# Second expert products a step behind the first, on fourteen weight slots, with expert numbers on VectorE

## The chip, the core and the metric

The kernel runs on one core of one Trainium2 chip. The metric is device time in microseconds of one execution; the time before is the median of three runs. In the profile the engines are called PE (TensorE), DVE (VectorE), ACT (ScalarE), POOL (GpSimd) and SP (SyncE, which issues the weight loads).

## What is computed

Two decoder layers on 256 tokens of width 1024, in float32. Each layer has a mixer and then a channel mixer; the first layer's is dense, the second one's is a choice of two out of eight experts, and this change touches that one alone:

```python
def moe_swiglu(h, router_w, w1, w3, w2):
    logits = (h @ router_w).astype(jnp.float32)
    top_v, top_i = lax.top_k(logits, TOP_K)
    probs = jax.nn.softmax(top_v, axis=-1)
    gates = jnp.sum(jax.nn.one_hot(top_i, N_EXPERTS, dtype=jnp.float32) * probs[..., None], axis=-2)
    y = jnp.zeros_like(h)
    for e in range(N_EXPERTS):
        y = y + gates[..., e:e + 1] * swiglu(h, w1[e], w3[e], w2[e])
    return y
```

`swiglu` is `(silu(h @ w1) * (h @ w3)) @ w2`, with 2816 inner columns. A last RMS norm with the gain `final_g` follows.

## The kernel before, in words

**Places.** The experts are sorted by how many tokens chose them, expert 0 first. Places 0 to 2 (`WIDE = 3`) have 128 slots, places 3 to 6 have 64, place 7 has 32. Tokens beyond these would go through a slow branch at the end that does not run here. Which expert stands at a place is a number that `place` works out (L861 to L892), on GpSimd in seventeen small steps, and that SyncE reads into a register before it can load that place's weights (`of_place`, L914).

**Units and slots.** Each expert's weights are 33 units of 128 x 2048 floats, 1 MiB each: 11 of w1, 11 of w3, 11 of w2. `load` (L134) takes a slot from a rotating list of tiles and issues the unit's DMA on SP; SP issues in order, so a load that waits for its slot holds all later ones. At the start of the expert stage the list `once` gives fifteen slots for one use each: three of pool `ahead`, four of `more`, six of `rawp`, tile `xn` and tile `big`. After them only `more` and `rawp` rotate, ten slots. The memory of `ahead` becomes the activations `a_hi` and `a_lo` of all 22 inner blocks of one wide expert, `xn` becomes the scatter's tile and `big` the activations of a narrow expert.

**Wide and narrow.** For a wide place each half unit is split into two parts of reduced precision, `whi` by ACT (L145) and `wlo` by DVE (L146), and each block of the product is three matmuls (`mm3`, L157 to L159): a unit is twelve matmuls of 512 columns. The unit's slot is free when the second `wlo` is done. A narrow place uses the raw unit (L1050, L1099), two matmuls side by side on the columns of the array; its slot is free when PE has used it.

**Steps.** `steps(p)` gives an expert's work: six inner steps (`inner`, four units each, the last two; then `turn`, which transposes the 512 new columns and writes the activations), then three outer steps (`outer`) of four, four and three units of w2, and after the last `scatter`, which multiplies by the gate and adds the rows back to the residual `xs`. The string `TURNS` says whose turn it is: 0 is a step of the wide stream (places 0 to 2), 1 one of the narrow stream (3 to 7). What follows a step's products (`turn`, `prepare` for the next place, `scatter`) is written after the products of the next turn. Within this order a scheduler sets each engine's own sequence. `prepare` gathers a place's tokens by a one-hot product (L973) and modulates them; `HOLD_E` names how many splits may stand ahead of which of its steps.

**The end.** After the last step `last_norm` squares, takes the row norm and multiplies by the gain row `fgt` (L1223), and two DMAs write the output. The gain row is fetched by `last_gain`, behind the third wide expert's scatter.

## Time and profile before

| | |
|---|---|
| median of three runs | 1168.63 us (1168.21 to 1170.08) |
| the profiled execution | 1168.7 us, its span 1166.9 us, mean granted clock 0.979 |
| busy share of the span | PE 95%, weight loads on PE 64%, DVE 54%, ACT 44%, POOL 3% |
| moved by DMA | 395.69 MB, 339 GB/s over the span |

The span goes from the first instruction to the last; the time of an execution is 1.8 us longer. In the profile each group of instructions has its line in the kernel, its engine, its operation and its tiles; `raw` is a weight unit, `x_hi`, `x_lo` and `x_n` are gathered tokens, `po` and `pb` hold outer products. A busy PE need not be PE at its peak, since the ends of matmuls are modelled; two starts in a row tell its pace better. The expert stage begins at about 467 us and lasts to the end.

### The profile page before, as it was taken

What the parts mean: (1) busy time and instruction counts of PE and PEld (TensorE: products, weight loads), DVE (VectorE), ACT (ScalarE), POOL (GpSimd) and SP (SyncE); (2) the same over time, 40 slices, a digit from 0 to 9 for tenths busy, and PEclk for the clock granted to TensorE, in tenths of its full rate; (3) what the DMA queues carried; (4) which work ended last, traced back from release to release, by engine and by line L of the source; (5) the groups of instructions that cost most, each with busy time, mean ns of one, the idle gap of its engine ahead of it and who ended that gap; (6) DMA issues with size and microseconds to landing.
All of it is one profiled execution on the core that took longest, in us unless ns stands there. A gap on an engine that the chain in (4) does not pass through costs nothing.

```text
span 1166.9 us, 15801 instructions
## 1 busy us (share of the span) xinstructions
PE 1107.4 (95%) x6125; PEld 742.8 (64%) x6125; DVE 627.4 (54%) x818; ACT 518.3 (44%) x724; POOL 30.5 (3%) x69
## 2 busy tenths in 40 slices
PE   4899999999999999899999999999999999998993
PEld 2578779999777888686465445554455544655540
DVE  2668556757776765797135443353343633345442
ACT  2764444444437744786234333542342333434331
POOL 2000000000001000300000000000000000000000
PEclk9899999999999999899999999999999999998996
DMA  9977486858886447495999999999999999999994
GB/s 361 410 288 291 145 324 249 310 201 306 334 332 229 147 143 288 181 359 189 418 420 419 420 419 420 419 420 420 388 406 419 420 419 419 419 419 403 398 420 172
DMA packets 57182, 395.69 MB, mean 339 GB/s; under 512 B 8294, under 2 KB 8710, under 8 KB 9356
## 3 DMA queue, kind: packets, MB, share of 16 engines
q1 hardware_dynamic: 54272, 393.24, 84.2%
q10 hardware_dynamic: 2828, 1.37, 0.4%
q8 instruction: 50, 0.82, 0.3%
q14 instruction: 32, 0.26, 0.1%
HBM read 393.53 MB, written 1.05 MB: 338 GB/s over the span
## 4 chain that ended last, share of the span: by engine, by line
PE 88%; DMA 4%; ACT 3%; DVE 2%; POOL 1%; issue 1%; ACTq 0%; POOLq 0%; DVEq 0%; SPq 0%
PE pa L1050 17%; PE pa L158 8%; PE pa L157 8%; PE pa L159 8%; PE po L1099 7%; PE pa L406 6%; PE pa L407 6%; PE pa L408 6%; PE pb L158 4%; PE pb L159 4%; PE pb L157 4%; PE pm L226 2%; PE pb L261 2%; PE pm L973 2%; DMA bdx<-in_wx_dram 2%; ACT whi L145 2%
## 5 line engine op out<-in xcount | busy, mean ns | idle before, releaser
L146 DVE TENSOR_TENSOR wlo<-raw,whi 128x1024 fp32r<-128x1024 f32 x318 | 378.6, 1222 | 205.1 <-ACT whi L145 204.4
L145 ACT ACTIVATE whi<-raw 128x1024 fp32r<-128x1024 f32 x318 | 324.5, 1057 | 214.7 <-PE pa L407 90.2
L1050 PE MATMUL pa<-raw,x_n 128*64 128x512 f32 (+3 forms) x960 | 205.0, 562 | 0.0
L406 PE MATMUL pa<-wide_hi,whi 128*128 128x256 f32 x544 | 154.3, 284 | 0.2 <-DVE wide_hi L380 0.2
L407 PE MATMUL pa<-wide_lo,whi 128*128 128x256 f32 x544 | 153.5, 282 | 0.2 <-DVE wide_lo L381 0.2
L408 PE MATMUL pa<-wide_hi,wlo 128*128 128x256 f32 x544 | 153.5, 282 | 0.0
L1050 PEld LDWEIGHTS pa<-raw,x_n 128*64 128x64 f32 (+1 forms) x960 | 63.0, 131 | 106.7 <-issue 101.3
L158 PE MATMUL pa<-wlo,x_hi 128*128 128x512 f32 (+1 forms) x288 | 113.3, 394 | 3.7 <-DVE wlo L146 3.7
L157 PE MATMUL pa<-whi,x_hi 128*128 128x512 f32 (+1 forms) x288 | 110.7, 389 | 0.9 <-ACT whi L145 0.3
L159 PE MATMUL pa<-whi,x_lo 128*128 128x512 f32 (+1 forms) x288 | 109.9, 382 | 0.1
L406 PEld LDWEIGHTS pa<-wide_hi,whi 128*128 128x128 f32 x544 | 102.3, 188 | 6.4 <-issue 4.0
L407 PEld LDWEIGHTS pa<-wide_lo,whi 128*128 128x128 f32 x544 | 102.5, 189 | 1.6 <-issue 1.1
L408 PEld LDWEIGHTS pa<-wide_hi,wlo 128*128 128x128 f32 x544 | 102.5, 188 | 0.3 <-issue 0.3
L1099 PE MATMUL po<-raw,big 128*64 128x512 f32 (+1 forms) x440 | 93.4, 616 | 6.3 <-DMA raw<-in_m_dram 6.3
L1053 ACT ACTIVATE s<-pa 128x512 f32<-128x512 f32 (+1 forms) x30 | 16.9, 562 | 163.4 <-PE pa L1050 163.4
L158 PE MATMUL pb<-wlo,a_hi 128*128 128x512 f32 x176 | 71.6, 408 | 2.0 <-DVE wlo L146 2.0
L158 PEld LDWEIGHTS pa<-wlo,x_hi 128*128 128x128 f32 x288 | 55.3, 192 | 26.5 <-DVE wlo L146 6.7
L159 PE MATMUL pb<-whi,a_lo 128*128 128x512 f32 x176 | 69.8, 398 | 0.0
L157 PEld LDWEIGHTS pa<-whi,x_hi 128*128 128x128 f32 x288 | 55.3, 192 | 21.8 <-issue 7.7
L157 PE MATMUL pb<-whi,a_hi 128*128 128x512 f32 x176 | 60.8, 403 | 2.0 <-ACT whi L145 2.0
L1099 PEld LDWEIGHTS po<-raw,big 128*64 128x64 f32 (+1 forms) x440 | 25.4, 132 | 57.8 <-issue 49.8
L159 PEld LDWEIGHTS pa<-whi,x_lo 128*128 128x128 f32 x288 | 55.5, 193 | 10.0 <-DVE x_lo L986 0.8
(323 smaller groups left out, 1242.4 us busy)
## 6 DMA issues: line engine op xcount, KB each, us to landing
raw<-in_m_dram SPq DMA_DIRECT2D x263, 1024.0 KB, 10.6
raw<-in_ada_w_dram SPq DMA_DIRECT2D x48, 1024.0 KB, 7.3
raw<-in_f_dram SPq DMA_DIRECT2D x33, 1024.0 KB, 6.0
raw<-in_win_dram SPq DMA_DIRECT2D x20, 1024.0 KB, 6.3
raw<-in_wout_dram SPq DMA_DIRECT2D x8, 1024.0 KB, 6.1
xs<-in_x_dram SPq DMA_DIRECT2D x1, 1024.0 KB
big<-in_m_dram SPq DMA_DIRECT2D x1, 1024.0 KB
out_dram<-big SPq DMA_DIRECT2D x2, 512.0 KB, 3.2
```

What stands on the lines that cost most here:

```text
L145: act.activation(hi[:, :n], src, AF.Copy)
L146: dve.tensor_tensor(lo[:, :n], src, hi[:, :n].bitcast(F32), op=ALU.subtract)
L157: pe.matmul(ps, l_hi, r_hi, start=first, stop=False)
L158: pe.matmul(ps, l_hi, r_lo, start=False, stop=False)
L159: return pe.matmul(ps, l_lo, r_hi, start=False, stop=last)
L226: return pe.transpose(o, i, ident[:i.shape[0], :i.shape[0]])
L261: pe.matmul(ps[o:o + 32, :], cact[:, k, :], wi[:, h * 512:(h + 1) * 512], start=(j == 0), stop=(j == 3))
L406: pe.matmul(pv[:, b, :], wh, h_hi[:, k, :], start=(k == 0), stop=False)
L407: pe.matmul(pv[:, b, :], wh, h_lo[:, k, :], start=False, stop=False)
L408: pe.matmul(pv[:, b, :], wl, h_hi[:, k, :], start=False, stop=(k == KD - 1))
L1050: pe.matmul(ps[r:r + m, :n], x_n[:, k, :], w[:, kk * n:(kk + 1) * n], start=(k < js), stop=(k >= KD - js))
L1099: pe.matmul(acc[r:r + m, :], aa["a_n"][:, k, :], w[:, i * 1024 + c * 512:i * 1024 + (c + 1) * 512], start=(k < js), stop=(k >= KF - js))
```

## The change

The outer product of 512 inner columns follows the inner step that made them by one step of its stream: `steps` now goes inner 0, inner 1, outer 0, inner 2, outer 1 and so on to outer 5, and `outer` takes two units (the last one). Activations are kept by step, in two buffers each, so that the memory of all 22 blocks goes to weight slots: fourteen rotate from the first load on, seven of `more`, six of `rawp` and `xn`. `TURNS` has 96 turns for 72, and both streams end together. The number of each place is worked out on DVE in eight steps that stand behind the second `t_lo`. One-hot tiles share a tile with the scatter, whose two halves share it too; the gain row takes the memory of `x_lo`.

```diff
-MORE = 4
-AHEAD = 3
+MORE = 7
-HOLD_E = (0, 2, 1, 1, 1)
+HOLD_E = (0, 1, 1, 1, 1)
-TURNS = "00000" + "110" * 18 + "10" * 4 + "11111"
+TURNS = "00000" + "110" * 28 + "10" * 3 + "1"
...
-    cmf = const([P, P], F32, "cmf", pre)
+    cmf = pre.tile([P, P], F32, tag="dg0", name="cmf")
...
-        once.extend([ahead] * AHEAD + [more] * MORE + [rawp] * RAW_BUFS)
-        once.append(lambda: cst.tile([P, 2048], F32, tag="xn", name=nm("raw")))
-        once.append(lambda: et([P, 2048], "big"))
-        pools[:] = [more] * MORE + [rawp] * RAW_BUFS
+        pools[:] = [more] * MORE + [rawp] * RAW_BUFS + [lambda: cst.tile([P, 2048], F32, tag="xn", name=nm("raw"))]
...
-        def place():
+        def place(behind):
...
+            with tc.issue_after(behind.ins):
+                dve.scalar_tensor_tensor(key[:], cnt_ps[:, :NE], float(NE), idx[:], op0=ALU.mult, op1=ALU.subtract)
+                dve.memset(key[:, 0:1], 2.0 * SEQ * NE)
+                dve.tensor_tensor(m[:], key[:].unsqueeze(1).to_broadcast(sq), key[:].unsqueeze(2).to_broadcast(sq),
+                                  op=ALU.is_gt)
+                dve.tensor_reduce(rank[:], m[:], axis=AX.X, op=ALU.add)
+                dve.tensor_tensor(m[:], rank[:].unsqueeze(1).to_broadcast(sq), idx[:].unsqueeze(2).to_broadcast(sq),
+                                  op=ALU.is_equal)
+                dve.tensor_tensor(eq[:], m[:], idx[:].unsqueeze(1).to_broadcast(sq), op=ALU.mult)
+                dve.tensor_reduce(number[:], eq[:], axis=AX.X, op=ALU.add)
+                last = dve.tensor_copy(number_i[:], number[:])
...
-            pool.tensor_scalar(key[:], cnt[:], float(NE), None, op0=ALU.mult)
...
-            pool.tensor_copy(number_i[:], summed(eq))
...
-            oh = et([P, NT, 2, P], "oh", F32R)
+            oh = et([P, NT, 2, P], "ob", F32R)
...
-                    dst = et([P, 2, P], "h32", bufs=2)[:] if wide_place(p) else x_hi[:, k:k + 2, :]
+                    dst = wk.tile([P, 2, P], F32, tag="s", name=nm("h"))[:] if wide_place(p) else x_hi[:, k:k + 2, :]
...
+                inners[p, c] = a_n = et([P, 4, m], "a_n", bufs=2)
...
+            inners[p, c] = a_hi, a_lo = [et([P, 4, P], h, F32R, bufs=2) for h in ("a_hi", "a_lo")]
...
-        def outer(e, units, acc):
+        def outer(e, c, acc):
+            units = range(2 * c, min(2 * c + 2, 11))
+            inn = inners.pop((e, c))
...
-            ob = cst.tile([P, NT, D], F32R, tag="xn", name=nm("ob"))
-            def parts(i, src, gate):
-                o_hi, o_lo = ob[:, i, 0:512], ob[:, i, 512:1024]
+            def parts(src, gate):
+                ob = et([P, 2, 512], "ob", F32R)
+                o_hi, o_lo = ob[:, 0, :], ob[:, 1, :]
...
-            fgt = aa["pool"].tile([P, NT, D], F32, tag="a_lo", name="fgt")
+            fgt = et([P, D], "x_lo")
...
-            for c in range(6):
-                a = inner(p, c)
...
-            for units in ((0, 1, 2, 3), (4, 5, 6, 7), (8, 9, 10)):
-                acc = outer(p, units, acc)
+            for c in range(7):
+                if c < 6:
+                    a = inner(p, c)
...
+                    yield rest_of
+                if c:
+                    acc = outer(p, c - 1, acc)
...
+        pools[:] = [pl for pl in pools if not callable(pl)]
+        fin = cst.tile([P, NT, D], F32, tag="xn", name="fin")
```

On SP, the loads at the start of the expert stage. `raw` numbers rise in the order of use; `raw627` is the first unit before and `raw629` after. Before the change:

```order
L134 DMA raw627_4511<-in_m1_dram 128x2048
L134 DMA raw632_4533<-in_m3_dram 128x2048
L134 DMA raw637_4555<-in_m1_dram 128x2048
L134 DMA big730_4950<-in_m1_dram 128x2048
L134 DMA raw725_4928<-in_m3_dram 128x2048
L134 DMA raw735_4972<-in_m3_dram 128x2048
L134 DMA raw744_5006<-in_m1_dram 128x2048
L134 DMA raw749_5028<-in_m3_dram 128x2048
L134 DMA raw754_5050<-in_m1_dram 128x2048
L134 DMA raw759_5072<-in_m3_dram 128x2048
L914 TENSOR_LOAD number_i612_4441
```

The same place on SP after the change:

```order
L129 DMA raw629_4501<-in_m1_dram 128x2048
L129 DMA raw634_4523<-in_m3_dram 128x2048
L129 DMA raw639_4545<-in_m1_dram 128x2048
L129 DMA raw644_4567<-in_m3_dram 128x2048
L129 DMA raw652_4594<-in_m1_dram 128x2048
L129 DMA raw657_4616<-in_m3_dram 128x2048
L129 DMA raw662_4638<-in_m1_dram 128x2048
L129 DMA raw723_4891<-in_m1_dram 128x2048
L129 DMA raw728_4913<-in_m3_dram 128x2048
L129 DMA raw734_4938<-in_m2_dram 128x2048
L129 DMA raw739_4960<-in_m2_dram 128x2048
L896 TENSOR_LOAD number_i614_4426
```

Five loads of later units stand ahead of the first unit in both. Before, the first three units come eleventh to thirteenth and twenty wide units are loaded ahead of the number that the narrow places need; after, the first seven come sixth to twelfth, there are sixteen, and the first w2 units (`in_m2`) are among them.

On DVE, the steps between the second `t_lo` and the first splits of the expert stage, before the change:

```order
L958 SCALAR_TENSOR_TENSOR t_lo585_4360<-xs_81,r32_1606_4416,t_hi584_4359 128x1024
L146 TENSOR_TENSOR wlo629_4514<-raw627_4511,whi628_4513 128x1024
L146 TENSOR_TENSOR wlo631_4524<-raw627_4511,whi630_4523 128x1024
L985 CAST x_hi613_4446<-h32616_4457 128x256
L986 TENSOR_TENSOR x_lo614_4447<-h32616_4457,x_hi613_4446 128x256
L146 TENSOR_TENSOR wlo634_4536<-raw632_4533,whi633_4535 128x1024
L985 CAST x_hi613_4446<-h32618_4471 128x256
L857 TENSOR_TENSOR pe_611_4430<-pm_610_4429,pos598_4395 128x64
L986 TENSOR_TENSOR x_lo614_4447<-h32618_4471,x_hi613_4446 128x256
```

The same place on DVE after the change:

```order
L940 SCALAR_TENSOR_TENSOR t_lo585_4357<-xs_81,r32_1606_4413,t_hi584_4356 128x1024
L861 SCALAR_TENSOR_TENSOR key609_4421<-pm607_4417,idx602_4400 128x8
L862 MEMSET key609_4421 128x1
L863 TENSOR_TENSOR pm_611_4423<-key609_4421 128x64
L865 TENSOR_REDUCE prank610_4422<-pm_611_4423 128x8
L867 TENSOR_TENSOR pm_611_4423<-prank610_4422,idx602_4400 128x64
L869 TENSOR_TENSOR pe_612_4424<-pm_611_4423,idx602_4400 128x64
L870 TENSOR_REDUCE number613_4425<-pe_612_4424 128x8
L871 CAST number_i614_4426<-number613_4425 128x8
L141 TENSOR_TENSOR wlo631_4504<-raw629_4501,whi630_4503 128x1024
```

The eight steps that make the numbers now stand ahead of the first split; before, DVE met their result at the first `pe`, behind the third split.

On PE, the last products and the scatters behind them. Before, the last narrow place's w2 units stand alone:

```order
L1099 MATMUL po1600_8869<-raw1610_8915,big1492_8410 32x512 x4
L1099 MATMUL po1600_8869<-raw1611_8921,big1492_8410 32x512 x4
L1099 MATMUL po1600_8869<-raw1612_8927,big1492_8410 32x512 x4
L1099 MATMUL po1600_8869<-raw1613_8933,big1492_8410 32x512 x4
L1099 MATMUL po1600_8869<-raw1614_8939,big1492_8410 32x512 x4
L1155 MATMUL pm1617_8950<-ob1615_8945,oht1410_8030 128x512
```

PE at the same place after the change; `pb` and `whi` belong to the last wide place:

```order
L152 MATMUL pb1418_7883<-whi1664_8938,a_hi1643_8862 128x512
L1073 MATMUL po1537_8398<-raw1666_8954,a_n1656_8913 32x512 x4
L153 MATMUL pb1417_7882<-wlo1665_8939,a_hi1643_8862 128x512
L154 MATMUL pb1417_7882<-whi1664_8938,a_lo1644_8863 128x512
L153 MATMUL pb1418_7883<-wlo1665_8939,a_hi1643_8862 128x512
L154 MATMUL pb1418_7883<-whi1664_8938,a_lo1644_8863 128x512
L1118 MATMUL pm1669_8965<-ob1667_8960,oht1285_7329 128x512
L1118 MATMUL pm1670_8969<-ob1667_8960,oht1285_7329 128x512
L1119 MATMUL pm1669_8965<-ob1667_8960,oht1285_7329 128x512
```

The wide place's last unit and its scatter (L1118, L1119) moved to the end, ahead of the narrow scatter.

## Rows read from the trace of the kernel before

**Rows 1.** The page, part 1: busy us, share of the span, instructions.

```profile
PE 1107.4 (95%) x6125; PEld 742.8 (64%) x6125; DVE 627.4 (54%) x818; ACT 518.3 (44%) x724; POOL 30.5 (3%) x69
```

**Rows 2.** Stretches: length, busy us by engine, granted clock, DMA share, GB/s.

```profile
480.00:500.00 20.00, 19.09 (x79) 14.48 (x79) 15.39 (x37) 16.12 (x21) 5.38 (x16) 0.90 0.22 80
500.00:560.00 60.00, 60.00 (x286) 43.02 (x286) 44.35 (x46) 42.42 (x60) 0.00 (x0) 1.00 0.76 287
560.00:820.00 260.00, 257.18 (x1212) 139.37 (x1209) 107.61 (x127) 94.14 (x137) 0.00 (x0) 1.00 1.01 419
820.00:880.00 60.00, 58.86 (x282) 32.40 (x280) 24.19 (x32) 22.31 (x34) 0.00 (x0) 1.00 0.98 398
880.00:1060.00 180.00, 176.74 (x793) 92.52 (x792) 80.49 (x86) 65.08 (x86) 0.00 (x0) 0.99 1.01 419
1060.00:1100.00 40.00, 35.77 (x186) 22.74 (x186) 19.25 (x24) 18.87 (x26) 0.00 (x0) 0.95 0.96 392
```

**Rows 3.** The page, part 6: expert loads, KB each, median us to landing.

```profile
raw<-in_m_dram SPq DMA_DIRECT2D x263, 1024.0 KB, 10.6
big<-in_m_dram SPq DMA_DIRECT2D x1, 1024.0 KB
```

**Rows 4.** Waits of the DMA queue, 470 to 560: us, times, longest.

```profile
SPq L134 <- DVE wlo L146: 37.4, 13, 10.1
SPq L134 <- DVE pe L857: 22.6, 1, 22.6
```

**Rows 5.** SP in order of time: start us, us, loads merged.

```profile
495.85 0.33 SPq L134 DMA_DIRECT2D raw<-in_m_dram  x1
...
500.86 51.92 SPq L134 DMA_DIRECT2D raw<-in_m_dram  x14
```

**Rows 6.** PE by group, 481.6 to 552.4: busy us, mean ns, idle before.

```profile
L158 PE MATMUL pa<-wlo,x_hi 128*128 128x512 f32 x80 | 33.0, 413 | 0.6 <-DVE wlo L146 0.6
...
L157 PE MATMUL pa<-whi,x_hi 128*128 128x512 f32 x80 | 31.4, 407 | 0.2 <-DVE x_hi L985 0.2
```

**Rows 7.** PE in order of time: start us, us, what.

```profile
481.65 0.73 PE L157 MATMUL pa<-whi,x_hi 128*128 128x512 f32 x1
...
541.21 0.40 PE L159 MATMUL pa<-whi,x_lo 128*128 128x512 f32 x1
...
541.91 0.39 PE L159 MATMUL pa<-whi,x_lo 128*128 128x512 f32 x1
...
547.54 1.08 PE L1050 MATMUL pa<-raw,x_n 128*64 128x512 f32 x4
548.55 0.50 PE L158 MATMUL pa<-wlo,x_hi 128*128 128x512 f32 x1
```

**Rows 8.** DVE in order of time, at the numbers: idle before in brackets.

```profile
486.66 0.23 DVE L857 TENSOR_TENSOR pe<-pm,pos 128x64 f32<-128x64 f32 x1 [4.39 <-POOL number_i L891]
```

**Rows 9.** PE in order of time, one round of narrow and wide steps.

```profile
689.86 7.08 PE L1050 MATMUL pa<-raw,x_n 128*64 128x512 f32 x30
...
719.12 7.08 PE L1050 MATMUL pa<-raw,x_n 128*64 128x512 f32 x30
```

**Rows 10.** All engines in order of time, behind the last landing.

```profile
1149.16 1.94 PE L1099 MATMUL po<-raw,big 128*32 128x512 f32 x8 [0.64 <-DMA raw<-in_m_dram]
1151.15 0.69 DVE L1130 TENSOR_TENSOR o<-po,gate_n 128x512 f32<-128x512 f32 x1 [15.51 <-PE po L1099]
1151.88 0.63 ACT L1131 ACTIVATE ob<-o 128x512 fp32r<-128x512 f32 x1 [15.55 <-DVE o L1130]
1152.54 0.69 DVE L1132 TENSOR_TENSOR ob<-o,ob 128x512 fp32r<-128x512 f32 x1 [0.69 <-ACT ob L1131]
...
1154.24 1.41 DVE L1137 SCALAR_TENSOR_TENSOR xs<-pm,gates_p,xs 128x512 f32<-128x512 f32 x2 [1.01 <-PE pm L1155]
...
1155.57 1.40 DVE L1137 SCALAR_TENSOR_TENSOR xs<-pa,gates_p,xs 128x512 f32<-128x512 f32 x2
```

**Rows 11.** Splits, 560 to 1149: busy us, mean ns, idle before and releasers.

```profile
L146 DVE TENSOR_TENSOR wlo<-raw,whi 128x1024 fp32r<-128x1024 f32 x154 | 180.0, 1221 | 122.9 <-ACT whi L145 122.5
L145 ACT ACTIVATE whi<-raw 128x1024 fp32r<-128x1024 f32 x154 | 152.3, 1055 | 56.1 <-DMA raw<-in_m_dram 36.1 <-PE pa L159 11.4 <-PE pb L159 8.4
```

More of the change, by code (lines that the diff above doesn't have):

```diff
@@ L118, in trunk @@
     pools = [rawp]
-    once = []
     last_load = []
     def slot():
-        if once:
-            pl = once.pop(0)
-        else:
-            pl = pools.pop(0)
-            pools.append(pl)
+        pl = pools.pop(0)
+        pools.append(pl)
         if callable(pl):
@@ new lines, in place @@
+            m, eq = (ep.tile(sq, F32, tag=n_, name=nm(n_)) for n_ in ("pm_", "pe_"))
+            number, number_i = et([P, NE], "number"), et([P, NE], "number_i", I32)
+            with tc.issue_after(behind.ins):
[9 more added lines that the diff above has]
+                last = dve.tensor_copy(number_i[:], number[:])
@@ L1003, in turn @@
                 ti = transpose(tv[:, b, :], a[:, b * P:(b + 1) * P])
-            o = slice(4 * c, 4 * c + n)
-            if not aa:
-                first.close()
-                ap_ = ctx.enter_context(tc.tile_pool(name="inner", bufs=1, side="right", reuse_waits="tile"))
-                aa["pool"] = ap_
-            if c == 0 and wide_place(p):
-                for h in ("a_hi", "a_lo"):
-                    aa[h] = aa["pool"].tile([P, KF, P], F32R, tag=h, name=nm(h))
             if not wide_place(p):
                 m = slots(p)
-                if c == 0:
-                    aa["a_n"] = et([P, KF, m], "big")
+                inners[p, c] = a_n = et([P, 4, m], "a_n", bufs=2)
                 g = wk.tile([P, 4, m], F32, tag="s", name=nm("g"))
@@ L1189, in steps, with rest_of @@
-            acc = None
-            for units in ((0, 1, 2, 3), (4, 5, 6, 7), (8, 9, 10)):
-                acc = outer(p, units, acc)
-                def rest_of(u=units[-1], acc=acc):
-                    if u == 10:
-                        scatter(p, acc)
-                        if p == WIDE - 1:
-                            last_gain()
-                yield rest_of
+            acc = None
+            for c in range(7):
+                if c < 6:
+                    a = inner(p, c)
+                    def rest_of(c=c, a=a):
+                        turn(p, c, a)
+                        if p == 0 and c == 1:
+                            place_rest()
+                            gate_halves(aa["last"])
+                            prepare((WIDE, WIDE + 1))
+                        if c == 5 and wide_place(p) and p + 1 < WIDE:
+                            prepare((p + 1,))
+                        if c == 5 and not wide_place(p) and (p - WIDE) % 2 and p + 1 < NE:
+                            prepare(tuple(range(p + 1, min(p + 3, NE))))
+                    yield rest_of
+                if c:
+                    acc = outer(p, c - 1, acc)
+                    def rest_of(c=c, acc=acc):
+                        if c == 6:
+                            scatter(p, acc)
+                            if p == WIDE - 1:
+                                last_gain()
+                    yield rest_of
@@ L1253, in experts @@
                     oht = turned(oh, F32)
-                    aT = aa["pool"].tile([P, KF, P], F32, tag="a_hi", name=nm("aT"))
+                    acc = [pb(), pb()]
                     for c in range(6):
@@ L1273, in experts @@
                             transpose(tv[:, b, :], a[:, b * P:(b + 1) * P])
-                        act.activation(aT[:, 4 * c:4 * c + nb, :], tv[:, :nb, :], AF.Copy)
-                    acc = [pb(), pb()]
-                    for u in range(11):
-                        w = load(of_place(m2, e, u))
-                        for i in range(2):
-                            k = 2 * u + i
-                            for c in range(2):
-                                pe.matmul(acc[c][:], aT[:, k, :], w[:, i * 1024 + c * 512:i * 1024 + (c + 1) * 512],
-                                          start=(k == 0), stop=(k == KF - 1))
+                        aT = et([P, 4, P], "a_hi", bufs=2)
+                        act.activation(aT[:, :nb, :], tv[:, :nb, :], AF.Copy)
+                        for u in range(2 * c, min(2 * c + 2, 11)):
+                            w = load(of_place(m2, e, u))
+                            for i in range(2):
+                                k = 2 * u + i
+                                for q in range(2):
+                                    pe.matmul(acc[q][:], aT[:, k % 4, :], w[:, i * 1024 + q * 512:i * 1024 + (q + 1) * 512],
+                                              start=(k == 0), stop=(k == KF - 1))
                     for c in range(2):
```

74 lines of the change are left out of this document (21 added, 53 removed).

## The prediction

> **What bounds the kernel now.** I read the page first, then a table of stretches, then the DMA queue's own waits, then single rows. The page shows two engines near their limit: PE is busy 95% of the span, and the weights that it multiplies arrive by DMA at rates that the next view shows [rows 1]. The table of stretches tells where the expert stage loses transfer time. From 560 to 820 and from 880 to 1060 the queue moves 419 GB/s at a full share; from 480 to 500 it moves 80, from 500 to 560 it moves 287, from 820 to 880 it moves 398 and from 1060 to 1100 it moves 392 [rows 2]. All expert weights come in units of 1024 KB, 264 of them (263 into stream slots, one into another tile) [rows 3]. At 419 GB/s one unit takes 1.0486 MB / 419 GB/s = 2.50 us, so the 264 take 660 us: nearly the whole expert stage. I therefore take the transfers as the bound from 560 us on, and the question is how much transfer time the start of the stage loses, what is lost later, and what follows the last landing.
>
> Why the start loses it: between 470 and 560 us SyncE waits 37.4 us for the splits' subtraction and 22.6 us once for a later one of VectorE's small steps [rows 4], which means for slots. Fifteen loads are out by 473; the next goes out at 495.85, and after one more fourteen follow from 500.86 to 552.8 [rows 5], so that the thirty-first, the last of these, leaves at 552.4. In this stretch PE is the limit: it never idles from 500 to 560 [rows 2]. Between 481.6 and 552.4 it runs 240 wide products, three lines of 80 of which two are shown [rows 6]: twenty wide units of twelve. Four wide products in a row start from 541.21 to 541.91, 0.233 us apart [rows 7], so the twenty units alone are 56 us of these 71.
>
> **The change, part by part.** (1) *The start.* Five wide steps still come first, but they are now inner 0, inner 1, outer 0, inner 2, outer 1: 4+4+2+4+2 = 16 units and not 20. The thirty-first load is the one to compare. Before, it takes the slot of the twenty-first unit, the first narrow one: the first three slots are never used again and ten rotate. After, fourteen slots rotate from the start, so it takes the slot of the seventeenth unit, which is again the first narrow one. Both kernels have thirty loads out when PE finishes its first narrow unit, and PE gets there four wide units earlier: 48 products x 0.233 = **11.2 us**. The narrow steps read weights much faster than the queue brings them, so from there on the queue is full, as it is from 560 on now. Ends: 12.0, if the 0.8 us that PE idles in the stretch for splits and first activations [rows 6] goes too; 8.4, if one of the four units (2.8 us) is still waited for in another way. I take 11.2.
>
> (2) *Later losses.* 60 us x (1 - 398/419) = 3.0 and 40 x (1 - 392/419) = 2.6: 5.6 us in the two stretches in which ten slots were not enough [rows 2]. Four more slots are 10 us more lead, against gaps of at most 5 us. In the stretches where the lead was enough nothing was lost, and those are the nearest rows, so I take all of it, **-5.6**; the ends are -5.6 and +5.6, the latter if the smaller steps make as many new gaps as they close.
>
> (3) *The numbers on VectorE.* Before, VectorE stands 4.39 us at 486.66 for the last of seventeen GpSimd steps [rows 8]. After, eight small steps of about 0.23 us (the row at 486.66 has such a one) stand on VectorE ahead of the first split: 1.8 us. Behind them wait the first splits and the first activations, and for those PE; but PE's first wide product starts only at 481.65 [rows 7], behind its gathers, and PE idled 0.8 us in the whole stretch although VectorE stood still for 4.39. So neither the stall nor its removal is on PE's path: 0, between +1.8 and -0.8. GpSimd has nothing else to do there. SyncE reads the numbers ahead of the seventeenth load and not the twenty-first; they are there at about 479.5, and that load cannot leave before the third unit's slot is free, near 490: 0.
>
> (4) *Order of products.* No product, load or split is added or removed. Outer steps have two units, so there are 96 steps for 72, and 24 more changes between wide and narrow work on PE. At 547.54 four narrow instructions stand between wide products, and the next wide one starts 1.01 us later [rows 7]; in a run of thirty, 7.08 us [rows 9], four take 0.94. With the slower start of the wide product itself I estimate 0.1 to 0.3 us for a change, 2 to 7 us in all, spread over 590 beside transfers: 0 as long as the queue is the bound. If it is not, it is the second rival's price. Activations of an outer step are made two steps earlier, so nothing waits for them in the listing.
>
> (5) *Buffers that change name* (one-hot tiles with the scatter's tile, modulated blocks with the small work tiles, the causal mask's source with a norm tile): these steps lie on VectorE and ScalarE, which are busy 54% and 44% of the span [rows 1], and ahead of PE by a step: 0; uncovered it would be about 0.7 us, one step of VectorE on 512 columns [rows 10], for each of the eight modulated blocks of the second and third expert.
>
> (6) *The end.* Before, the last five steps are narrow and the wide stream is long done. After, the last wide unit lands one unit (2.5 us) ahead of the last narrow one, and two scatters stand behind the last landing, the wide one's two halves on a single tile. Now: the last unit's products start at 1149.16 and the residual is complete at 1155.57 + 1.40 = 1156.97, so 7.8 us [rows 10]. After, counted from the last landing: the wide unit's two halves need two ScalarE copies of 1.06 and a subtraction of 1.22 [rows 11], so the second low part is there 2 x 1.06 + 1.22 - 2.5 + 0.1 = 0.95 us after it; four products and their drain, 1.3; then on VectorE fourteen steps of 0.70 (three gate products, three low parts, eight additions [rows 10]) = 9.8, less none that can run beside each other, and 0.65 for the first copy. Sum 12.7, so **+4.9**. Ends: +3, if the first gate product starts when its own half is done and the additions close up; +9, if PE, which waits there now and takes 1.94 us for the last unit [rows 10], runs all its products behind the landing at that pace. The final gain's row moves with the wide scatter: its transfer is issued on ScalarE's queue about seven units ahead of the last landing, and its one multiplication stands on ScalarE ahead of the first copy, in the 2 us in which ScalarE waits for the wide products. That hides it; if the row lands later, what is missing is paid, and the +9 covers it. From the complete residual to the end nothing changes: 1166.9 - 1157.0 = 9.9.
>
> *Sum.* The profiled execution took 1168.7 us for a span of 1166.9, the median of the three runs is 1168.63, so there is no correction: 1168.7 - 11.2 - 5.6 + 0 + 4.9 = **1156.8 us**. With one term at a time at its end it is 1154.9 (the end at +3) to 1160.9 (the end at +9), the upper end of (2) apart, which is rival A.
>
> **Rivals.** *A: the lead is given back.* At its first narrow unit PE is now fourteen units behind the queue and not ten, and it gains on the queue only slowly: a round of eight narrow and four wide units goes from the run of narrow products at 689.86 to the one at 719.12, 29.3 us [rows 9], against 12 x 2.50 = 30.0. Then every place where wide work bunches makes the queue wait again, and (2) ends at +5.6: 1168.7 - 11.2 + 5.6 + 4.9 = 1168.0, no change. Against it: the same thin margin kept the queue full for 260 us in one piece. Chance 0.13.
>
> *B: PE becomes the bound, and the kernel is slower.* The margin is 0.7 us in 30. If the 24 more changes, each 0.3, and waits for splits take it, the queue waits for PE all the way to the last expert; the order then moves no PE work away, the start gains nothing, and the end's 4.9 and up to 7 us of changes are added: 1168.7 + 4.9 + 7 = 1180.6, or 1173.6 without the changes. It decides when twelve units take PE over 30.0 us. For it speaks PE's 95% [rows 1]; against it that ScalarE's copies stood 36.1 us for landings between 560 and 1149 [rows 11], which a stream that waits for PE does not show. Chance 0.10. The Trainium skill's page Perfetto Trace Analysis, in its section Identifying the Most-Contended Engine, says that the matmul busy share is no good measure of how near PE is to its limit and names the weight loads' share in its place. By that rule PE is at 64% here, rival B falls away and its 0.10 would go to the forecast; the full DMA rows agree with it, but the round above does not leave PE a third of its time, so I keep B.
>
> *C: more than that.* The first refill leaves near 481 and not at 495.85, and if PE's own waits shrink with the longer lead, (1) is 12 and the end is at its lower price +3, with a further 2 us from PE's waits for splits: 1168.7 - 12 - 5.6 + 3 - 2 = 1152. Chance 0.10.
>
> That the change does not do what it says is excluded for the order by the listing; what is left of it is A.
>
> **How the numbers follow.** Forecast 0.67, A 0.13, B 0.10, C 0.10. The likeliest is 1156.8. The range for 8 in 10 goes from 1151, just under C, to 1167, where A begins; left out are B, most of A and a little below C. Faster or slower by under 0.2% (2.3 us, about what a measurement of this kernel can tell from no change) goes to A's middle: faster 0.67 + 0.10 + 0.03 of A = 0.80, the same 0.08 of A, slower 0.10 + 0.02 of A = 0.12.
>
> **What would show it.** Right: the refill after the first fourteen loads leaves at about 481; the thirty-first load leaves near 541; 419 GB/s from 550 on without a weak stretch; the last landing near 1132; two scatters behind it and about 12.7 us to the complete residual. Wrong: weak stretches after 560 (A); SyncE waiting for PE through the middle and ScalarE no longer waiting for landings (B); PE idle before its first narrow product, or a last landing later than 1138 (the start's term); a tail of over 18 us, if the gain row or the half clock stands in it.

## The result and the profile after

The changed kernel takes 1156.74 us, median of 4 runs (1155.28 to 1158.61); the kernel before took 1168.89 beside it. The ratio is 0.9896, with a 95% interval from 0.9884 to 0.9909. The profiled execution took 1157.38 us for a span of 1155.6. Part 1 of its page answers to [rows 1]:

```profile
PE 1100.3 (95%) x6125; PEld 739.3 (64%) x6125; DVE 628.5 (54%) x826; ACT 517.2 (45%) x724; POOL 21.7 (2%) x52
```

The same 6125 products keep PE busy 7.1 us less than before. The table of stretches answers to [rows 2] (length, busy us by engine, granted clock, DMA share, GB/s):

```profile
443.00:480.00 37.00, 32.82 (x175) 27.94 (x174) 21.88 (x52) 17.56 (x30) 2.85 (x13) 0.91 0.79 313
480.00:500.00 20.00, 20.00 (x84) 16.77 (x84) 18.70 (x42) 17.48 (x23) 0.00 (x0) 0.83 0.74 266
500.00:560.00 60.00, 60.00 (x283) 40.52 (x281) 37.58 (x38) 38.91 (x56) 0.00 (x0) 1.00 0.87 339
560.00:820.00 260.00, 258.91 (x1208) 136.90 (x1207) 109.33 (x128) 93.10 (x136) 0.00 (x0) 1.00 1.01 419
820.00:880.00 60.00, 59.30 (x290) 32.46 (x289) 23.28 (x24) 22.04 (x30) 0.00 (x0) 1.00 1.01 420
880.00:1060.00 180.00, 175.59 (x853) 92.92 (x852) 80.20 (x97) 65.47 (x97) 0.00 (x0) 1.00 1.01 419
1060.00:1100.00 40.00, 35.26 (x194) 19.18 (x195) 19.53 (x22) 18.42 (x25) 0.00 (x0) 1.00 1.01 420
```

I turn these rates into transfer time lost: length x (1 - rate/419). Up to 560 it is 9.4 + 7.3 + 11.5 = 28.2 us. Before it was 8.1 + 16.2 + 18.9 = 43.2, from [rows 2] and from the stretch 443 to 480, which stood there at

```profile
443.00:480.00 37.00, 33.43 (x178) 28.63 (x176) 22.23 (x46) 18.54 (x31) 6.29 (x14) 0.91 0.82 327
```

So the start gave back **15.0 us**. The two weak stretches at 820 and 1060 are full now and gave back the other 5.6. The waits of the DMA queue from 470 to 560 answer to [rows 4] (us, times, longest):

```profile
SPq L129 <- DVE wlo L141: 37.9, 14, 4.6
SPq L129 <- PE pa L747: 17.1, 1, 17.1
SPq L129 <- PE pa L1022: 13.0, 8, 6.2
SPq L129 <- DVE past L889: 9.3, 1, 9.3
```

The one long hole (22.6) is now 9.3 and the longest wait for a split went from 10.1 to 4.6. The 17.1 belong to the slot that is the router's tile until then. The loads in order of time (start, length of the stretch, loads) show that ten go out from 472.62 to 507; before there were fifteen out by 473, and the next one left at 495.85 [rows 5]:

```profile
472.62 34.59 SPq L129 DMA_DIRECT2D raw<-in_m_dram  x10
...
533.12 7.94 SPq L129 DMA_DIRECT2D raw<-in_m_dram  x3
...
539.89 11.47 SPq L129 DMA_DIRECT2D raw<-in_m_dram  x9
```

The end answers to [rows 10]. The last load is issued at 1108.4 and lands 21.1 us later, so at about 1129.4; the rows are for the last six loads (issue to landing, min/median/max):

```profile
L129 SPq DMA_DIRECT2D raw<-in_m_dram x6: 333/333/333, 1095.9 to 1108.4; - x6
DMA to landing us min/median/max: 19.8/20.0/21.1
```

and all engines in order of time around it:

```profile
1120.28 0.73 PE L152 MATMUL pb<-whi,a_hi 128*128 128x512 f32 x2 [1.31 <-ACT whi L140]
1121.54 0.79 PE L153 MATMUL pb<-wlo,a_hi 128*128 128x512 f32 x1 [0.53 <-DVE wlo L141]
1122.12 0.63 PE L154 MATMUL pb<-whi,a_lo 128*128 128x512 f32 x1
1122.55 0.63 PE L153 MATMUL pb<-wlo,a_hi 128*128 128x512 f32 x1
...
1126.97 2.01 ACT L140 ACTIVATE whi<-raw 128x1024 fp32r<-128x1024 f32 x2 [3.76 <-DMA raw<-in_m_dram]
1128.06 2.36 DVE L141 TENSOR_TENSOR wlo<-raw,whi 128x1024 fp32r<-128x1024 f32 x2 [3.03 <-ACT whi L140]
...
1134.42 1.29 DVE L1104 TENSOR_TENSOR o<-pb,gate_f 128x512 f32<-128x512 f32 x2 [4.01 <-PE pb L154]
...
1144.25 1.40 DVE L1111 SCALAR_TENSOR_TENSOR xs<-pa,gates_p,xs 128x512 f32<-128x512 f32 x2
```

The residual is complete at 1145.65, **16.2 us** behind the last landing; before it was 7.8. The ledger from these rows is -15.0 - 5.6 + 8.4 = -12.2. The medians differ by 12.15, but the two profiled executions, from which the rows come, by 1168.7 - 1157.38 = 11.3, so the ledger is 0.9 us too large: the last landing moved from about 1149.1 to 1129.4, by 19.7 us and not 20.6. Rates in whole GB/s allow that much, since 1 GB/s over 260 us is 0.6 us.

### The profile page after: what moved, and what is told of

Read it like the earlier page. It is cut to its first block, busy times and chain, and to the rows that moved or that the text cites. A ratio compares the mean times of both kernels' runs of the same rounds, so it can differ in the third digit from the quotient of the medians.

```text
span 1155.6 us, 15809 instructions
## 1 busy us (share of the span) xinstructions
PE 1100.3 (95%) x6125; PEld 739.3 (64%) x6125; DVE 628.5 (54%) x826; ACT 517.2 (45%) x724; POOL 21.7 (2%) x52
## 4 chain that ended last, share of the span: by engine, by line
PE 86%; DMA 6%; DVE 3%; ACT 3%; issue 1%; POOL 0%; POOLq 0%; SPq 0%; ACTq 0%
PE pa L1022 15%; PE pa L153 8%; PE pa L152 8%; PE pa L154 8%; PE po L1073 8%; PE pa L401 6%; PE pa L402 6%; PE pa L403 6%; PE pb L153 4%; PE pb L152 4%; PE pb L154 4%; DMA raw<-in_m_dram 3%; PE pm L221 2%; PE pm L955 2%; DVE wlo L141 1%; DMA bdx<-in_wx_dram 1%
## 5 line engine op out<-in xcount | busy, mean ns | idle before, releaser
L1022 PE MATMUL pa<-raw,x_n 128*64 128x512 f32 (+3 forms) x960 | 193.3, 560 | 0.6 <-DMA raw<-in_m_dram 0.6
L1073 PE MATMUL po<-raw,a_n 128*64 128x512 f32 (+1 forms) x440 | 98.4, 603 | 0.0
L152 PEld LDWEIGHTS pa<-whi,x_hi 128*128 128x128 f32 x288 | 55.4, 192 | 21.1 <-issue 7.2
L261 DVE SCALAR_TENSOR_TENSOR acc<-raw,cs,acc 128x1024 f32<-128x1024 f32 x37 | 47.4, 1281 | 11.6 <-DMA raw<-in_ada_w_dram 7.9
```

The lines of the kernel that those rows point to most:

```text
L152: pe.matmul(ps, l_hi, r_hi, start=first, stop=False)
L261: dve.scalar_tensor_tensor(acc[:], wi, cs[:, k:k + 1], acc[:], op0=ALU.mult, op1=ALU.add)
L1022: pe.matmul(ps[r:r + m, :n], x_n[:, k, :], w[:, kk * n:(kk + 1) * n], start=(k < js), stop=(k >= KD - js))
L1073: pe.matmul(acc[r:r + m, :], inn[:, k % 4, :], w[:, i * 1024 + c * 512:i * 1024 + (c + 1) * 512], start=(k < js), stop=(k >= KF - js))
```

## The experiments

All edits are to the changed kernel, and all times are medians; the kernel before had 1168.1 to 1168.9 beside them. "Lost" is the transfer time worked out as above.

### Slots without the order undone

```diff
-MORE = 7
+MORE = 3
```

> Edit: the changed kernel with ten stream slots instead of fourteen (MORE 3 for 7); the order of the steps stays. Theory (slots and order both carry the gain): when TensorE reaches its first narrow unit at about 541 us, four loads fewer are out than with fourteen slots, 4 x 2.50 = 10.0 us of transfer, and the weak stretches in the middle of the stage come back (in the kernel before they cost 5.6). The last landing moves from 1129.4 to 1139.4 without and 1145.0 with the dips; TensorE is then no longer behind at the end, so the tail is the predicted 12.7 and not the 16.2 of the changed kernel: 1163.5 to 1169 us in all, and the table of stretches shows less than 419 GB/s somewhere after 560. Rival (the order alone brought the gain, slots are only margin): 1156 to 1158.5, no weak stretch.

1171.07 us, ratio to the kernel before 1.0032 (1.0022 to 1.0043): the new order with ten slots is slower than the old kernel. The stretches:

```profile
443.00:480.00 37.00, 32.82 (x175) 27.82 (x174) 21.88 (x52) 17.57 (x29) 2.85 (x13) 0.93 0.52 200
...
560.00:820.00 260.00, 256.36 (x1182) 134.93 (x1182) 107.27 (x126) 92.50 (x136) 0.00 (x0) 1.00 1.01 414
820.00:880.00 60.00, 59.29 (x268) 29.14 (x265) 24.23 (x24) 21.54 (x27) 0.00 (x0) 1.00 1.01 419
```

With 262 and 332 GB/s in the next two stretches it loses 39.3 us up to 560, 11.1 more than the changed kernel, and 260 x (1 - 414/419) = 3.1 after it: 14.2 of the 14.3 measured. The rival falls. What I had not expected: the old weak stretches at 820 and 1060 stay full with ten slots; others open between 660 and 820. So the order had closed the old two, and the slots close those that the order opens. The tail did not shrink to 12.7 either: the last landing is at 1143.2 and the span ends at 1168.9, 9.95 of it behind the complete residual, so it is 15.8, and the time lies over the expected range.

The next edit keeps fourteen slots, but lets four of them be used once:

```diff
-MORE = 7
+MORE = 3
+AHEAD = 4
...
-        pl = pools.pop(0)
-        pools.append(pl)
+        if once:
+            pl = once.pop(0)
+        else:
+            pl = pools.pop(0)
+            pools.append(pl)
...
+        ahead = ctx.enter_context(tc.tile_pool(name="ahead", bufs=AHEAD, side="right", reuse_waits="tile"))
+        once.extend([ahead] * AHEAD)
```

> Edit: the changed kernel with its fourteen slots, but four of the first ones are used once only and ten rotate, which is how the kernel before had its slots (five once, ten rotating); the order of steps stays. It tells what of the start is the order's and what the rotation's. Theory (the queue's loss up to 560 is set by when slots come back): the first fourteen loads go as in the changed kernel, 10.8 us lost by 480; the fifteenth waits for the fifth wide unit's slot, so up to 560 it loses as much as with ten slots, 39 to 41 us against 29.5, and the weak stretches cost 3.5 as there: 1156.7 + 10.5 + 3.5 = 1170.7, from 1168.5 to 1172. Rival (the order alone takes four wide units, 11.2 us, off the start, as the prediction put it): about 1157 to 1162.

1168.99 us, ratio 1.0006 (0.9996 to 1.0016): the new order on slots that work like the old ones is worth nothing. Its stretch from 480 and its loads in order of time:

```profile
480.00:500.00 20.00, 20.00 (x84) 16.78 (x84) 18.71 (x42) 17.47 (x23) 0.00 (x0) 0.83 0.17 56
```

```profile
472.63 34.59 SPq L134 DMA_DIRECT2D raw<-in_m_dram  x6
```

Against the changed kernel's ten loads from the same moment to the same moment these are six: each slot event lets a load go that is four units earlier in the list. Four units of 2.50 are 10.0 us, and the loss up to 560 is 9.4 + 17.3 + 11.5 = 38.2, 10.0 more. That is 5.0 less than the kernel before, which is about the order's own part of the start; it is not exact, since this kernel has four slots for one use and the kernel before has five, and the numbers are on VectorE here. The rival (the order alone takes 11.2) falls.

### How many wide steps come first

```diff
-TURNS = "00000" + "110" * 28 + "10" * 3 + "1"
+TURNS = "000000" + "110" * 29 + "10" + "1"
```

> Edit: the changed kernel with six wide steps first instead of five, that is 20 wide units ahead of the first narrow one, as many as in the kernel before; fourteen slots stay, the tail keeps the order wide, narrow, wide, narrow, narrow nearly (110 110 10 1 for 10 10 10 1). Theory (the start pays by wide units, 12 x 0.233 = 2.8 us each): first narrow load and last landing 11.2 us later, near 1140.6; TensorE, which in the changed kernel is 5.0 us behind the last landing, is then not behind, so 3.5 us come back in the tail: 1164.5, plus or minus 2. Rival one (the simple sum of the prediction): 1156.7 + 11.2 = 1168. Rival two (TensorE is the bound in the changed kernel, its work is the same in any order): 1155.5 to 1158.5, with the last landing later but TensorE's last product near 1134.

1166.03 us (ratio 0.9982, 0.9971 to 0.9993), near the theory's 1164.5, but by another way. The stretches that differ:

```profile
500.00:560.00 60.00, 60.00 (x276) 41.73 (x274) 41.82 (x41) 41.06 (x58) 0.00 (x0) 1.00 0.83 309
...
880.00:1060.00 180.00, 174.47 (x834) 92.27 (x837) 78.96 (x93) 63.82 (x92) 0.00 (x0) 1.00 1.00 408
```

Up to 560 it loses 32.6 us, 4.4 more than with five steps, and 4.9 after that. So four wide units at the start cost 4.4 us and not 11.2: while the slots rotate, each wide unit hands one back, and the queue only runs at 309 to 340 GB/s instead of 419. The other 4.9 are weak stretches that this order opens, which none of this run's theories had.

```diff
+TURNS = "000" + "110" * 26 + "10" * 7 + "1"
```

> Edit: the changed kernel with three wide steps first instead of five, that is 10 wide units ahead of the first narrow one and not 16 (000, 26 times 110, 7 times 10, 1). Theory (the queue is the bound, each wide unit at the start lets it wait): in the changed kernel the queue loses 3.0 us from 500 to 520, 7.1 to 540 and 1.4 to 560; 7 to 10 of these 11.5 go, the last landing comes at 1120 to 1122.5 and the time is 1147 to 1150. Rival (TensorE is as near to its bound as the queue: it idles some 17 us in the whole stage, and its products are the same in any order): the queue's gain only makes loads wait for TensorE, SyncE's waits grow in the middle, ScalarE waits no longer for landings, and the time is 1153.5 to 1158. Third (the thinner lead opens weak stretches later, as six wide steps first did for 5.6 us): rates under 419 after 560 and 1156 or more.

1163.58 us (0.9957, 0.9941 to 0.9972), far above the theory and the rival. The third allows the time, but not by its reason: the stretches after 560 cost only 1.0 us (418 GB/s in two of them). The stretch from 443 and the longest wait of the DMA queue from 440 to 560 say why:

```profile
443.00:480.00 37.00, 32.82 (x174) 27.66 (x173) 21.41 (x48) 18.05 (x28) 2.84 (x13) 0.94 0.50 203
```

```profile
SPq L896 <- DVE number_i L871: 25.0, 1, 25.0
```

Only the first expert's weights can be asked for without a number. With three wide steps first the eleventh load is already another expert's, and SyncE stands 25.0 us for the number with free slots in hand. It loses 19.1 by 480, where the changed kernel loses 9.4, and wins some of that back by 560: all its losses together are 4.3 us above the changed kernel's, and its last landing is that much later (issued at 1112.3 and landed at 1133.7). The rest lies behind the landing. The residual is complete 19.9 us after it, at 1153.56 (16.2 in the changed kernel), and PE is late there: from 560 to 1149 ScalarE's splits wait for no landing, only for PE (8.9 us idle before them):

```profile
L140 ACT ACTIVATE whi<-raw 128x1024 fp32r<-128x1024 f32 x166 | 165.4, 1053 | 8.9 <-PE pa L154 7.1 <-PE pb L154 1.7
```

```diff
+TURNS = "0000" + "110" * 27 + "10" * 5 + "1"
```

> Edit: the changed kernel with four wide steps first (0000, 27 times 110, 5 times 10, 1): 14 units of the first expert, exactly the fourteen slots, ahead of the first load that needs an expert's number. With three steps first SyncE stood 25.0 us for the numbers at the eleventh load and the queue lost 9.2 us more by 480; here the first load that needs one is the fifteenth, which waits for a slot until 482 anyway. Theory: no such loss; two wide units fewer take 2.0 to 2.5 us off the queue's loss up to 560 (four more cost 4.3), so 1154.4, from 1153.5 to 1156. Rival (TensorE or the lead is the limit now, as three or six steps first suggest: weak stretches after 560 of 3 us or more): 1157 to 1160.

1158.28 us (0.9912, 0.9896 to 0.9929): the rival's time, but not by its weak stretches. From 443 to 500 nothing is lost beside the changed kernel (313 and 263 GB/s), then:

```profile
500.00:560.00 60.00, 60.00 (x289) 37.67 (x289) 33.09 (x32) 34.68 (x52) 0.00 (x0) 1.00 0.83 328
```

13.0 lost against 11.5. The queue waits there once 10.2 us for a narrow unit's slot (6.2 in the changed kernel): narrow units come earlier in the list of loads, and their slots come back only when PE gets to them. Three, four, five and six wide steps first give 1163.6, 1158.3, 1156.7 and 1166.0. The turns are 96 in each, so these orders differ in their last turns too. That a wide unit fewer always helps, which lay in the start's term, is refuted.

### Numbers on GpSimd

The edit puts back the steps of `place()` as the kernel before had them.

```diff
-HOLD_E = (0, 1, 1, 1, 1)
+HOLD_E = (0, 2, 1, 1, 1)
...
-                numbered = place(ti)
+                place()
```

> Edit: the changed kernel with the expert numbers computed on GpSimd again, by the code of the kernel before. Theory (as predicted, no part of the gain): 1156 to 1158.5 us, first wide product and refill at the same time within 1 us. Rival (the transfer time won at the start was 14.7 us and not 11.2 because VectorE no longer stands 4.4 us for the numbers): refill and first splits 2 to 4 us later, and 1158.5 to 1161 us.

1156.13 us (0.9899, 0.9878 to 0.9920): not to be told from the changed kernel. VectorE stands for the number again, as in [rows 8]:

```profile
486.47 0.23 DVE L847 TENSOR_TENSOR pe<-pm,pos 128x64 f32<-128x64 f32 x1 [4.39 <-POOL number_i L881]
```

The queue moves less from 480 to 500 (218 for 266 GB/s) and more from 500 to 560 (352 for 339); both lose 28 to 29 us. This run also shows the tail without the half clock, which the section on the hardware takes up.

### The tail

```diff
+TURNS = "00000" + "110" * 26 + "10" * 5 + "111"
```

> Edit: the changed kernel with its last wide step moved two steps ahead, so that three narrow steps end the stage (10 10 10 10 10 111 for 110 110 10 10 10 1). The tail's term: in the changed kernel 16.2 us lie between the last landing at 1129.4 and the complete residual at 1145.65, because a wide unit, its scatter and a narrow scatter stand behind it. Theory (the wide scatter is what the tail costs, and TensorE is nearly the bound): TensorE still ends near 1134.5, then the narrow scatter alone, 5.9 us as in the kernel before: residual at 1140.4, so 1151.5 us in all, from 1150 to 1153. Rival one (the queue alone is the bound): last landing 1129.4 + 7.8 = 1137.2, so 1148.3. Rival two (what the end wins, steps bunched ahead of it lose as waits for splits): 1156 to 1158.

1155.30 us (0.9890, 0.9868 to 0.9911), 3.8 us over the theory's 1151.5 and just under the second rival's 1156. The wide scatter now runs ahead of the last narrow steps, but still over them. In order of time:

```profile
1129.17 0.39 PE L1022 MATMUL pa<-raw,x_n 128*32 128x256 f32 x3
...
1135.05 1.41 DVE L1111 SCALAR_TENSOR_TENSOR xs<-pm,gates_p,xs 128x512 f32<-128x512 f32 x2 [1.07 <-PE pm L1119]
...
1135.86 0.44 PE L221 MATMUL pm<-ident,s 128*128 128x128 f32 x2 [0.61 <-DVE xs L1111]
```

The products of the last inner block are done at 1129.6, but the transposes that must follow them stand in line behind the wide scatter and its additions until 1135.86. So I moved the wide steps further ahead:

```diff
+TURNS = "00000" + "110" * 24 + "10" * 7 + "11111"
```

> Edit: the changed kernel with its last wide step moved further ahead, so that five narrow steps end the stage as in the kernel before (24 times 110, 7 times 10, 11111). With three narrow steps at the end the wide scatter still held VectorE until 1136.5, and TensorE's last narrow inner block, whose products were done at 1129.4, had its transposes wait for that until 1135.9. Theory (the wide scatter is the tail's cost wherever it stands within two steps of the end): with five steps it is done before the last landing at 1130, and the residual is complete 7.8 us after the landing as before, at 1137.8; 1137.8 + 9.95 + 1.0 = 1148.7, from 1147.5 to 1150. Rival (TensorE is the bound, its products end near 1134 in any order, and the half clock at the end is paid): 1151.5 to 1154. Second rival (seven bunched wide steps make the queue wait): a weak stretch between 1000 and 1110 and 1153 or more.

1154.83 us (0.9887, 0.9866 to 0.9908): the theory's 1148.7 is missed by 6 us. ScalarE's splits now wait for no landing at all after 560 (their idle time there is 6.9 us, all for PE), the queue is as full as before, and PE is late:

```profile
1130.93 1.93 PE L1022 MATMUL pa<-raw,x_n 128*32 128x256 f32 x30
...
1133.74 2.78 PE L1073 MATMUL po<-raw,a_n 128*32 128x512 f32 x24
```

All weights have landed by 1129.6, but three units of the last outer step are multiplied from 1133.74 on, and the residual is complete at 1142.0. To see whether PE's products are the reason I left some out, with the five narrow steps and without:

```diff
-        pe.matmul(ps, l_hi, r_lo, start=False, stop=False)
+        mi = pe.matmul(ps, l_hi, r_lo, start=False, stop=last and not third)
+        if not third:
+            return mi
...
-                                    lo[:, kk * 512:(kk + 1) * 512], k == 0, k == KD - 1)
+                                    lo[:, kk * 512:(kk + 1) * 512], k == 0, k == KD - 1,
+                                    third=e < 2 or c < 3)
```

> Edit: the version with five narrow steps last (1154.8 us), with the same 9.3 us of TensorE's products left out (third product in the last wide expert's inner steps 3 to 5, so part of the result is only approximate). In that version ScalarE waits for no landing after 797 us, the last weights land about 1128.9 and the residual is complete at 1142.6, 13.7 us later and not 7.8 as in the kernel before. Theory (with the narrow tail TensorE has become the bound, which ate the queue's gain): the lag goes, the residual is complete about 7.8 to 9 us after the landing, 1148.9 to 1150 in all. Rival (a chain of VectorE and ScalarE steps behind the landing, not TensorE's products): 1154 to 1155.5.

1149.53 us (0.9831, 0.9814 to 0.9847), as the theory said. PE now waits for the last landing, and the end looks as in [rows 10]:

```profile
1129.80 1.93 PE L1077 MATMUL po<-raw,a_n 128*32 128x512 f32 x8 [1.51 <-DMA raw<-in_m_dram]
...
1136.21 1.40 DVE L1115 SCALAR_TENSOR_TENSOR xs<-pa,gates_p,xs 128x512 f32<-128x512 f32 x2
```

1129.80 to 1137.61 is 7.8 us, the same as before the change. So with a narrow tail PE's products are the limit at the end, and 9.3 us fewer of them are worth 5.3; beyond that the last landing is the limit again. A part of the 5.3 may be the clock: granted was 0.72 from 1105 to 1110 with all products and 1.00 with fewer.

> Edit: the changed kernel with the third of the three products left out in the last four to five wide inner blocks' worth of work: the last wide expert's inner steps 3, 4 and 5 (ten units, about 40 products of 0.233 us, 9.3 us of TensorE after about 1010 us). Part of the result is therefore only approximate. Loads, splits and order stay. Theory (in the changed kernel's own tail the landing of the last wide unit at 1127 and the chain behind it set the end, TensorE is 2.3 us late at most): 1154.4 to 1157. Rival (TensorE as a whole is late there): the residual is complete at 1129.4 + 12.7 = 1142.1 or earlier, 1153.2 or less.

1156.47 us (0.9895, 0.9879 to 0.9912), nothing: in the changed kernel's own order the last wide unit's landing and the chain behind it set the end, and PE's total does not.

The last run puts the two edits together that were each a little lower, five narrow steps last and the numbers on GpSimd:

> Edit: the changed kernel with five narrow steps last and the numbers on GpSimd, the two edits that each came out a little under the changed kernel (1154.8 and 1156.1 against 1156.7). If they add: 1154.2, from 1153.2 to 1155.5. If TensorE is the bound with the narrow tail, the place of the numbers cannot matter unless its first wide product starts earlier: 1154.8, within 0.8.

1156.20 us (0.9888, 0.9871 to 0.9904): they do not add. And with three wide steps first and five narrow ones last:

> Edit: both edits together on the changed kernel, three wide steps first and five narrow steps last (000, 22 times 110, 11 times 10, 11111). Theory with the queue as bound: last landing 1120 to 1122.5 plus 7.8 and 11: 1139 to 1142. With TensorE as bound: no better than five narrow steps last alone, 1147.5 to 1150. With new weak stretches: over 1150.

1165.97 us (0.9977, 0.9968 to 0.9987). It has the same stand for the number (194 GB/s from 443 to 480) and new weak stretches from 1000 on (408 and 405 GB/s). None of the complete kernels beats the changed one by more than its interval.

## Why the prediction came out

The time was right (1156.8 for 1156.74; the profiled execution took 1157.4), and that it was right to a microsecond is luck: two errors cancel. The last landing came at 1129.4 and not near 1132, and the tail behind it took 16.2 us and not 12.7.

- **The bound.** Right. With the changed kernel's tail, what the queue loses comes back in the time one for one, to a microsecond or so: ten slots lost 14.2 us more and cost 14.3, four slots used once 10.0 + 1.9 and 12.3, six steps first 9.3 and 9.3, four steps first 1.5 and 1.5. Three steps first is the exception, with 3.3 + 1.0 lost and 6.8 paid: its last landing is 4.3 us later, and the rest is paid in the tail, where PE is late.
- **Term 1, the start: 11.2 predicted, 15.0 measured.** The refill at 481 came at 482. Two counts were off. The thirty-first load, expected near 541, left at 533.1, and it was the thirty-second that waited for the first narrow unit, at 539.9: one load more was out than in the kernel before, 2.5 us. And PE reached that unit 552.4 - 539.9 = 12.5 us earlier, not 11.2. The sum of both is 15.0. The reasoning "four wide units fewer, 0.233 each product" also gave the gain to the wrong part of the change: about 5.0 us are the order's and 10.0 the rotation's.
- **Term 2, later losses: -5.6, right in size.** Its reason was wrong: I put it down to four more slots, but with ten slots the old weak stretches stay closed. The order closed them; it opens others, worth 3.1 us with ten slots and 1.9 with four used once, and these the slots close.
- **Term 3, numbers on VectorE: 0.** Right. The price of the number lies elsewhere: it is nothing at the seventeenth load, as the prediction said, and 25.0 us of SyncE at the eleventh.
- **Term 4, order of products: 0.** No cost is seen: PE's busy time fell by 7.1 us with the same products. It was not tried alone. **Term 5, buffers: 0.** Nothing in the runs speaks against it; it was not tried alone.
- **Term 6, the end: +4.9 predicted (12.7 us behind the last landing), +8.4 measured (16.2).** The step that failed is the stretch from the landing to the scatter's first step: 0.95 + 1.3 = 2.25 us predicted, while that step starts only at 1134.42, 5.0 us behind the landing. The low part was there as predicted, 1.0 us behind the landing (1128.06 + 2.36 = 1130.42); what was mis-sized are the products behind it, 1.3 predicted, for which VectorE stands 4.01 us. I had PE free at the landing. It was not: eight narrow products of about 1.0 us stand between wide ones, twice, and some eight wide products ran at half clock from 1121.5 on, so that PE came late. At full clock VectorE stands 2.29 us there, with the numbers on GpSimd (the same products, a tail of 13.9 us) and with the lighter products in the changed order alike. So of the missing 2.7 us about 1.7 (4.01 - 2.29) go with the half clock, and the other 1.0 is what the last eight narrow products take ahead of the last wide ones (1.06 us from 1132.66). The chain behind it was 10.45 predicted and 11.2 measured.
- **Rival A** (lead given back): no weak stretch after 560. It does appear with another start, six wide steps first. **Rival B** (PE becomes the bound): ScalarE still waits for landings, 9.8 us between 560 and 1149 against 36.1 [rows 11], so it did not come, but it is closer than that. With five narrow steps last it decides, and it takes 5.3 us (1154.83 against 1149.53). The Trainium skill's page Perfetto Trace Analysis (Identifying the Most-Contended Engine) would have let this rival fall by the weight loads' share, 64% of the span, which is one of the two measures that it names for PE, beside MFU (the share of PE's peak rate that the kernel's products use). That share is 64% in the five-narrow-steps kernel too, and 57% from 1000 to 1100, where the left-out products lie; leaving out 9.3 us of them gains 5.3. Here the measurement decides against this half of the rule, and the round of 29.3 in 30.0 us [rows 9] was the better sign.

## What to carry over

A slot that is used once costs the stream a whole unit of lead at the moment when the slow steps hand slots back; count loads out at the same instant in both kernels, and not only the time of one load. A leading block of slow steps has a best length on both sides: too short, and loads stand for a run-time index or for slots of steps not yet reached (1163.6 and 1158.3 us here; in the first PE is late at the end as well), too long, and the queue starves (1166.0). Where the transfers and the products of a stage differ by a few per cent, time won on one is kept only up to the other, and which of them decides can change with the order of the last few steps.

## What the runs showed of the hardware

The half clock in the tail comes and goes with the same work. In the changed kernel PE idled 1.31 and 0.53 us at 1120.28 and 1121.54 (shown above), and the wide products behind that stand 0.43 us apart, which is the lower of the two levels (1.2 GHz). With the numbers on GpSimd, PE meets the same place with idle times of 0.51 and 0.53, and stays at 0.23 us, the upper level (2.4 GHz). PE in order of time in that kernel, and two of VectorE's rows behind it:

```profile
1118.58 0.73 PE L152 MATMUL pb<-whi,a_hi 128*128 128x512 f32 x2 [0.51 <-ACT whi L140]
1119.84 0.51 PE L153 MATMUL pb<-wlo,a_hi 128*128 128x512 f32 x1 [0.53 <-DVE wlo L141]
1120.18 0.39 PE L154 MATMUL pb<-whi,a_lo 128*128 128x512 f32 x1
1120.41 0.40 PE L153 MATMUL pb<-wlo,a_hi 128*128 128x512 f32 x1
...
1133.31 1.29 DVE L1112 TENSOR_TENSOR o<-pb,gate_f 128x512 f32<-128x512 f32 x2 [2.29 <-PE pb L154]
...
1142.54 1.40 DVE L1119 SCALAR_TENSOR_TENSOR xs<-pa,gates_p,xs 128x512 f32<-128x512 f32 x2
```

The granted clock of the stretch 1120 to 1125 is 0.66 in the changed kernel and 1.00 there, and the tails take 16.2 and 13.9 us (there the last weights land at 1130.0 and the residual is complete at 1143.94). The idle time just before does not decide it, as two other runs show. With the lighter products in the changed order PE idles 1.31 and 0.53 us at this place, as in the changed kernel, and stays at 0.23 us:

```profile
1120.09 0.73 PE L152 MATMUL pb<-whi,a_hi 128*128 128x512 f32 x2 [1.31 <-ACT whi L140]
1121.35 0.50 PE L153 MATMUL pb<-wlo,a_hi 128*128 128x512 f32 x1 [0.53 <-DVE wlo L141]
1121.68 0.40 PE L156 MATMUL pb<-whi,a_lo 128*128 128x512 f32 x1
1121.92 0.39 PE L153 MATMUL pb<-wlo,a_hi 128*128 128x512 f32 x1
...
1132.88 1.29 DVE L1108 TENSOR_TENSOR o<-pb,gate_f 128x512 f32<-128x512 f32 x2 [2.29 <-PE pb L156]
```

With three wide steps first it idles 0.51 and 0.54, as with the numbers on GpSimd, and falls to 0.43 us:

```profile
1128.76 0.72 PE L152 MATMUL pb<-whi,a_hi 128*128 128x512 f32 x2 [0.51 <-ACT whi L140]
1130.02 0.50 PE L153 MATMUL pb<-wlo,a_hi 128*128 128x512 f32 x1 [0.54 <-DVE wlo L141]
...
1131.00 0.63 PE L154 MATMUL pb<-whi,a_lo 128*128 128x512 f32 x1
1131.43 1.06 PE L152 MATMUL pb<-whi,a_hi 128*128 128x512 f32 x2
```

The granted clock is 1.00 from 1120 to 1125 in the first of the two and 0.66 from 1130 to 1135 in the second. Why the clock falls in some executions and not in others the runs don't settle. It differs between executions of one kernel too: the four of the changed kernel, in the order of their mean granted clock over the span (0.983, 0.982, 0.981, 0.979), took 1155.28, 1156.09, 1157.38 and 1158.61 us. Whether it is this stretch that differs in them is not shown, since one of them alone was profiled; that 2.3 us of tail hardly show in the medians (1156.7 and 1156.1) fits it.
